# Extra weight slots that stay in the ring until the last outputs need them, and a read-back placed behind the last weight load

## The chip, the cores and the metric

One core of one Trainium2 chip runs the whole program in one launch. The metric is the time of the program on the device in microseconds; lower is better. The notes below call the engines by the profile's names: PE (matrix multiplies), DVE (vector), ACT (scalar), POOL, and SP, whose queue issues nearly all of the transfers here.

## The reference

A two-layer network over 256 tokens and 256 context tokens of width 1024. Each layer is a mixer (a gated linear attention, a Fourier mix and a windowed attention, merged) and then a mixture of 16 experts. Layer 0 works on tokens and context (512 rows), layer 1 on the tokens alone. What matters here is the mixture, and the start of the mixer that follows it:

```python
def hierarchical_moe(h, w_router_group, w_router_expert, w1, w3, w2):
    ...                                   # one group of four, two experts in it, their gates
    for e in range(MOE_EXPERTS):
        hid = jax.nn.silu(h @ w1[e]) * (h @ w3[e])
        out = out + (hid @ w2[e]) * gates[:, e:e + 1]
    return out
...
k_a, v_a, k_c, v_c, q_a, r_a, u_b, q_c, gate_logits = split_by(h @ w_in, IN_SIZES)
```

All weights are float32: an expert has 6 MB of them (`w1` and `w3` 1024 x 512, `w2` 512 x 1024).

## The kernel before, in words

In the mixture the experts stand in 16 places. Each place computes only the tokens that were routed to it: up to 128 rows in a big place ("B" in `PLACES`), up to 64 in a small one ("s"). The last two places, 14 and 15, are small in both layers. A big place splits its weights into a high and a low part on ACT and DVE; a small one multiplies the float32 weights as they are. The outputs of places 0 to 13 are scattered by an indirect DMA on POOL into a buffer `yb` in device memory. The outputs of the last two places stay on the chip, in the tiles `yes` that `last_y` takes; one-hot matmuls (`put_rows`, L1776) bring their rows to the tokens. `rows(t)` reads `yb` back for a block of 128 tokens (L1760), POOL adds its two halves (L1761), an identity matmul adds the sum to the same PSUM bank (L1779), and DVE multiplies by the gate (L1797) and adds the result to `x` (L1799). Layer 0 has four such blocks (t = 0 to 3), layer 1 two. Between the two halves of this lies a branch (`tc.If`, L1785) for the rare case that a place overflows; every engine loads the counter `cnti`, compares and jumps. In this run the branch isn't taken.

The weights come in pieces of 1 MB, six to a place, 96 to a layer, all issued from SP (`wload`, L245). `pieces_of` gives their order: for each place the second half of `w1` and of `w3`, then the first halves of the next place, then the two halves of `w2` of this one. So the last four pieces of a layer, 93 to 96, are the second halves of `w1` and `w3` of place 15 and its two pieces of `w2`; 91 and 92 are `w2` of place 14.

`ring` hands out the slot of the next piece in turn. The ring has 8 slots in layer 0 (9 in layer 1), two of them the tiles of the pool `raw`, which the mixer's own loads use too. `moe_ahead` adds four extra slots, so that there are 12 (13). With 12 slots in turn, pieces 91 and 92 stand in the two `raw` tiles of layer 0. In the kernel before, `ring` drops every extra slot that it meets once 84 pieces have been handed out (`CUT`), and the list `spare` gives the dropped slots to the last two outputs and the first two read-backs.

A tile is reused only when its last reader is done: the load into it waits on a semaphore, on SP, and SP issues in order. The order of the instructions on each engine is made by a scheduler from the program's order and its priorities; `behind` adds an edge that keeps one instruction after another on the same engine.

Of the kernel before, what the change touches and what calls it, by code (L numbers as in the profile page):

```python
# [8 lines left out]
F32 = mybir.dt.float32  # L9
F32R = mybir.dt.float32r  # L10
# [9 lines left out]
P = 128  # L20
# [10 lines left out]
RING = (6, 7)  # L31
ONCE = (0, 2)
AHEADG = 2
CUT = 84
EXTRA = 2
EA = 8
EB = 1
# [77 lines left out]
def ts(i, n):  # L115
    return slice(i * n, (i + 1) * n)
# [12 lines left out]
class Net:  # L129
# [468 lines left out]
    def mixer(self, l, filler):  # L598
        nc, io = self.nc, self.io
# [19 lines left out]
        if l:  # L619

            h = [hp.tile([P, 2, KD, SEQ], F32R, name=n) for n in ("hhi", "hlo")]
# [16 lines left out]
        s1 = ExitStack()  # L638
        yc = self.swa(s1)
        self.dump(f"y2{l}", yc[0].bitcast(F32))  # L640
        self.rings, self.ahead, self.slots, self.piece, self.gen = [], [], [], 0, self.pieces_of(l)
        if l:

            self.rings = [(Slot(self.x[:, 2:4].rearrange("p t d -> p (t d)")), False)]
# [1 line left out]
            n = EXTRA  # L646
# [4 lines left out]
        yb = self.fourier(s1)  # L651
# [610 lines left out]

    def ring(self):

        self.piece += 1
        if self.piece > CUT:

            while self.rings[0][1]:
                self.rings.pop(0)
        self.rings.append(self.rings.pop(0))  # L1270
        return self.rings[-1][0].tile([P, 2048], F32, name="wraw")

    def pieces_of(self, l):

        def src(w, q):
            if q < STAT[l]:
                return self.io[w][l, q]
            if q not in self.eid:
                self.eid[q] = self.nc.values_load(self.idi[0:1, q:q + 1], engines=(mybir.EngineType.SP,),
                                                  min_val=0, max_val=NE - 1)  # L1280
            return self.io[w][l][bass.ds(self.eid[q], 1)].rearrange("e r c -> (e r) c")

        def up(w, q, c):
            return (w, q, c), self.wload(src(w, q)[ts(c, 512), :], 4, 512, self.ring())

        def down(q):
            for c in range(2):
                yield ("w2", q, c), self.wload(src("w2", q)[ts(c, 256), :], 2, 1024, self.ring())

        def begin(q):  # L1290
            for w in ("w1", "w3")[:1 + (PLACES[l][q] == "s")]:
                yield up(w, q, 0)
        self.eid = {}
        yield from begin(0)
        for q in range(NE):
            yield up("w1", q, 1)
            if PLACES[l][q] == "B":
                yield up("w3", q, 0)
            yield up("w3", q, 1)
            if q + 1 == STAT[l]:  # L1300
                yield from down(q)
            if q + 1 < NE:
                yield from begin(q + 1)
            if q + 1 != STAT[l]:
                yield from down(q)
# [68 lines left out]
    def moe_ahead(self, l):  # L1374


        n = 2 - l
        y1 = self.pool(self.sd, "rb1", bufs=n, side="right")
        y0 = self.pool(self.sd, "rb0", bufs=n, side="right")

        self.spare = self.once[1:] + [y0] * n + [y1] * n + self.once[:1]
        self.rings[2:2] = [(p, True) for p in self.spare]
        gen = self.pieces

        first = [next(gen) for _ in range(len(self.rings) - ROWS[l].count("w"))]
        last = self.wd
        for o in ROWS[l]:
            if o == "w":
                with self.tc.issue_after(last.ins):
                    first.append(next(gen))  # L1390
                last = self.wd
            else:
                self.behind(self.hw[int(o)], last)
                last = self.hw[int(o)]
        self.pieces = chain(first, gen)
        self.got, self.cut, self.parts = {}, {}, 6
        self.cut["w1", 0, 0] = list(self.halves("w1", 0, 0))

    def moe(self, l):
        nc, io, tc = self.nc, self.io, self.tc  # L1400
# [4 lines left out]
        dp, h2b, yb, lg = self.dp, self.h2b, self.yb, self.lg  # L1405
# [33 lines left out]
        i = V.tensor_add(Mb, O[:, 0], O[:, 1])  # L1439
# [17 lines left out]
        for t in range(nt):  # L1457
            i = V.tensor_scalar(self.oh0[:, t], self.iotab[:, :cap], pm0[:, t:t + 1], None, op0=OP.is_equal)
# [209 lines left out]

        def last_y(e):

            ye = self.spare.pop(0).tile([P, 2048], F32, name="wraw").bitcast(F32R).rearrange("p (h d) -> p h d", h=2)
            yes.append(ye)
            return ye
        p1 = begin(0, xx)
        for e in range(NE):
# [33 lines left out]
            if e == NE - 2:  # L1709
# [9 lines left out]
                rq = self.pool(sr, "rows2", bufs=2, side="right") if nt > 2 else None  # L1719
            if not big[e]:  # L1720
                p2 = self.c2()
                for c in range(2):
                    w = self.piece_at("w2", e, c)
                    for k in range(2):
                        pair(p2, hs, [w[:, k:k + 1, ts(o, 512)] for o in range(2)], (2 * c + k, 4), 1)
                if e < NE - 2:
                    ye = yp.tile([P, 512], F32, name="ye")
                    nc.scalar.activation(ye, p2, AF.Copy, scale=gsl[:, e:e + 1])  # L1728
                    put = (ye, e)
                    continue  # L1730

                ye = last_y(e)[:, :, :512]
                nc.scalar.activation(ye[:, 0], p2, AF.Copy, scale=gsl[:, e:e + 1])
                V.scalar_tensor_tensor(ye[:, 1], p2, gsl[:, e:e + 1], ye[:, 0].bitcast(F32), op0=OP.mult, op1=OP.subtract)
                continue
# [7 lines left out]
            if e < NE - 2:  # L1743
                ye = yp.tile([P, D], F32, name="ye")
                for o in range(2):
                    nc.scalar.activation(ye[:, ts(o, 512)], p2[o], AF.Copy, scale=gsl[:, e:e + 1])
                put = (ye, e)
                continue
            ye = last_y(e)
            for o in range(2):  # L1750
                q = ts(o, 512)
# [4 lines left out]

        def rows(t):

            yr = (self.spare.pop(0) if t < 2 else rq).tile([P, 2048], F32, name="wraw").rearrange("p (r d) -> p r d", r=2)
            nc.sync.dma_start(yr, yb.rearrange("(r q) d -> q r d", r=2)[ts(t, P)])  # L1760
            i = nc.gpsimd.tensor_add(yr[:, 0], yr[:, 0], yr[:, 1])  # L1761
            self.adds += [i] if t >= 2 else []
            return yr
        self.adds, self.lates = [], []
        yrs = [rows(t) for t in range(nt)]

        def put_rows(t, pt, js):
# [16 lines left out]
        n = nc.values_load(cnti[0:1, 0:1], min_val=0, max_val=T)  # L1784
# [3 lines left out]
        for t in range(nt):  # L1788
            self.pri.append(tc.cur_priority)
            yr = yrs[t]  # L1790
# [6 lines left out]
            i = [V.tensor_mul(yr[:, 1, ts(o, 512)], pt[o], gb[:, t // 2, ts(o, 512)]) for o in range(2)]  # L1797
# [118 lines left out]
```

## Time and profile before

| | us |
|---|---|
| three runs | 1570.74, 1577.3, 1569.88 (median 1570.74) |
| the profiled execution | 1564.04 |
| its span, first to last instruction | 1562.3 |
| end of layer 0's mixture, last output matmul of place 15 | 926.25 |
| first projection matmul of layer 1 | 950.34 |

Times in the profile run from the start of the span. The profiled execution is 6.7 us below the median of the three runs, and 1.7 us above its own span. A row of a timeline has the start, the duration, the engine, the line of the kernel, the operation, the tiles as output <- inputs, the count of instructions merged in it, and in brackets how long the engine was idle before it and what ended that. A float32 matmul leaves two records.

### The profile page before, as it was taken

The page shows a single profiled execution, that of the slowest core. Times are in us where ns is not written, and L with a number is a line of the kernel's source. Part 1 is how long each engine was busy: PE and PEld are TensorE (multiplying, and loading weights), DVE is VectorE, ACT ScalarE, POOL GpSimd, SP SyncE. Part 2 cuts the span into 40 slices and gives each one's busy share as a digit, 9 for nine tenths or more (in the row PEclk, how much of TensorE's full clock was granted, in tenths as well). Part 3 has the DMA queues.
Part 4 walks back from the last instruction along what each step waited for, and adds up shares of the span by engine and source line. Part 5 has one row for each costly group of instructions (what it writes and reads, how often), then busy time and mean ns, then how long its engine had stood idle before and what let it go on. Part 6 is the DMA issues. An engine that isn't in the chain of part 4 may idle for free. (4 is left out here: it accounts for less than half of the span.)

```text
span 1562.3 us, 22623 instructions
## 1 busy us (share of the span) xinstructions
PE 1437.5 (92%) x8333; PEld 1029.9 (66%) x8333; DVE 937.5 (60%) x1757; ACT 746.8 (48%) x1286; POOL 214.0 (14%) x238
## 2 busy tenths in 40 slices
PE   6999899999999998899999979999899979998885
PEld 4666666677777798676665428687689967553521
DVE  4379767432366786897776327467965689341412
ACT  4568556422223232576665306668654448341411
POOL 1124100000111101111111014023001111021001
PEclk9999999999999998999999988999999989999998
DMA  9772242543556578799999863322335699999992
GB/s 325 205 222 92 95 152 68 182 134 122 175 188 203 189 226 317 248 348 379 394 378 385 303 242 118 130 84 82 98 109 185 216 339 334 378 386 394 395 360 120
DMA packets 230795, 363.17 MB, mean 232 GB/s; under 512 B 25676, under 2 KB 125206, under 8 KB 230676
## 3 DMA queue, kind: packets, MB, share of 16 engines
q1 hardware_dynamic: 223808, 349.77, 64.2%
q0 software_dynamic: 6432, 11.76, 2.1%
q8 instruction: 69, 1.13, 0.3%
q14 instruction: 50, 0.41, 0.1%
q10 hardware_dynamic: 436, 0.10, 0.0%
HBM read 350.56 MB, written 21.82 MB: 238 GB/s over the span
## 5 line engine op out<-in xcount | busy, mean ns | idle before, releaser
L266 DVE TENSOR_TENSOR wlo<-wraw,whi 128x1024 fp32r<-128x1024 f32 (+1 forms) x324 | 377.9, 1180 | 184.8 <-ACT whi L265 126.7
L265 ACT ACTIVATE whi<-wraw 128x1024 fp32r<-128x1024 f32 (+1 forms) x324 | 322.3, 1010 | 258.6 <-PE pa L229 110.4
L228 PE MATMUL pa<-hhi,whi 128*128 128x512 f32 (+1 forms) x704 | 240.0, 356 | 1.9 <-ACT qT L795 1.0
L229 PE MATMUL pa<-hlo,whi 128*128 128x512 f32 (+1 forms) x704 | 237.7, 352 | 0.0
L228 PEld LDWEIGHTS pa<-hhi,whi 128*128 128x128 f32 x704 | 133.3, 189 | 27.9 <-issue 10.0
L231 PE MATMUL pa<-hhi,wlo 128*128 128x512 f32 (+1 forms) x704 | 150.5, 349 | 0.0
L1646 PE MATMUL pa<-wraw,xh 128*64 128x512 f32 x520 | 147.2, 626 | 0.0
L229 PEld LDWEIGHTS pa<-hlo,whi 128*128 128x128 f32 x704 | 133.4, 190 | 19.4 <-issue 6.5
L231 PEld LDWEIGHTS pa<-hhi,wlo 128*128 128x128 f32 x704 | 113.5, 190 | 19.2 <-issue 4.8
L1659 DVE SCALAR_TENSOR_TENSOR th<-th,pa 64x512 f32<-64x512 f32 (+1 forms) x32 | 21.7, 679 | 122.6 <-ACT th L1658 122.5
L770 POOL TENSOR_TENSOR m<-m,gu 128x512 f32<-128x512 f32 (+1 forms) x32 | 37.5, 1171 | 403.9 <-DVE gu L768 403.9
L1646 PEld LDWEIGHTS pa<-wraw,xh 128*64 128x64 f32 x520 | 43.7, 142 | 74.4 <-issue 71.3
L235 PE MATMUL pa<-whi,xh 128*128 128x512 f32 x208 | 84.9, 408 | 3.8 <-ACT whi L265 3.7
L236 PE MATMUL pa<-wlo,xh 128*128 128x512 f32 x208 | 85.8, 413 | 1.5 <-DVE wlo L266 1.4
L237 PE MATMUL pa<-whi,xl 128*128 128x512 f32 x208 | 83.6, 402 | 0.1
L1646 PE MATMUL c<-wraw,hh 128*64 128x512 f32 x256 | 69.3, 631 | 1.0 <-DVE hh L1702 1.0
L236 PE MATMUL pa<-y,whi 128*128 128x512 f32 (+1 forms) x192 | 66.3, 345 | 0.9 <-DVE y L272 0.9
L1558 POOL DMA_INDIRECT xg<-h2b,tki x30 | 33.4, 1113 | 242.6 <-PE c L1630 75.1
L235 PE MATMUL pa<-y,whi 128*128 128x512 f32 (+1 forms) x192 | 65.4, 341 | 0.7 <-DVE mx L1150 0.7
L237 PE MATMUL pa<-y,wlo 128*128 128x512 f32 (+1 forms) x192 | 64.9, 338 | 0.0
L359 DVE SCALAR_TENSOR_TENSOR adaw<-adaw,cT 128x512 f32<-128x512 f32 x56 | 45.3, 809 | 25.1 <-DMA adaw<-in_w_ada_dram 24.4
L1564 POOL DMA_INDIRECT yb<-ye,yki x28 | 28.4, 1013 | 220.0 <-ACT ye L1728 111.5
(456 smaller groups left out, 2792.0 us busy)
## 6 DMA issues: line engine op xcount, KB each, us to landing
wraw<-in_w_dram SPq DMA_DIRECT2D x184, 1024.0 KB
wraw<-in_w_in_dram SPq DMA_DIRECT2D x44, 1024.0 KB
adaw<-in_w_ada_dram SPq DMA_DIRECT2D x80, 512.0 KB
adaw<-in_w_ada_dram SPq DMA_DIRECT2D x8, 1024.0 KB
wraw<-in_w_out_dram SPq DMA_DIRECT2D x8, 1024.0 KB
x<-in_w_dram SPq DMA_DIRECT2D x8, 1024.0 KB
yb<-zero SPq DMA_DIRECT2D x12, 512.0 KB
wraw<-yb SPq DMA_DIRECT2D x6, 1024.0 KB
```

The source lines that it names most:

```text
L228: mm(out, lh, rh, start=(i == 0), stop=False)
L229: mm(out, lh, rl, start=False, stop=False)
L231: self.mm = mm(out, ll, rh, start=False, stop=(i == len(ops) - 1))
L235: mm(out, lh, rh, start=start, stop=False)
L236: mm(out, lh, rl, start=False, stop=False)
L237: self.mm = mm(out, ll, rh, start=False, stop=stop)
L265: self.sp = nc.scalar.activation(hv[:, :, q], v[:, :, q], AF.Copy)
L266: self.sl = self.lo.tensor_sub(lv[:, :, q], v[:, :, q], hv[:, :, q].bitcast(F32))
L359: nc.vector.scalar_tensor_tensor(v[:, j], v[:, j], ck, acc, op0=OP.mult, op1=OP.add)
L770: nc.gpsimd.tensor_add(self.m[:, j, :], self.m[:, j, :], u[:, :TY])
L1558: return nc.gpsimd.indirect_dma_start(out=xgs[e % len(xgs)][:n], out_offset=None, in_=h2b, in_offset=bass.IndirectOffsetOnAxis(ap=tki[:n, ...
L1646: nc.tensor.matmul(ps[ts(i, SM)], xs[:, k0[0] + k, :], w[:, k, :], start=(k0[0] + k == 0), stop=(k0[0] + k == k0[1] - 1))
```

## The change

`CUT`, the counter `piece` and the list `spare` go. The extra slots stay in the ring, and a new method `leave` takes the first extra slot in the ring's order out of it when it is needed: once for each of the last two outputs, once for each of the first two read-backs. The read-back DMA gets an edge that keeps it behind the last weight load (`self.wd`) on SP.

```diff
-CUT = 84
...
     def ring(self):
-        self.piece += 1
-        if self.piece > CUT:
-
-            while self.rings[0][1]:
-                self.rings.pop(0)
         self.rings.append(self.rings.pop(0))
         return self.rings[-1][0].tile([P, 2048], F32, name="wraw")
+
+    def leave(self):
+
+        i = next(i for i, r in enumerate(self.rings) if r[1])
+        return self.rings.pop(i)[0].tile([P, 2048], F32, name="wraw")
...
-        self.spare = self.once[1:] + [y0] * n + [y1] * n + self.once[:1]
-        self.rings[2:2] = [(p, True) for p in self.spare]
+        self.rings[2:2] = [(p, True) for p in self.once[1:] + [y0] * n + [y1] * n + self.once[:1]]
...
-            ye = self.spare.pop(0).tile([P, 2048], F32, name="wraw").bitcast(F32R).rearrange("p (h d) -> p h d", h=2)
+            ye = self.leave().bitcast(F32R).rearrange("p (h d) -> p h d", h=2)
...
-            yr = (self.spare.pop(0) if t < 2 else rq).tile([P, 2048], F32, name="wraw").rearrange("p (r d) -> p r d", r=2)
-            nc.sync.dma_start(yr, yb.rearrange("(r q) d -> q r d", r=2)[ts(t, P)])
+            yr = (self.leave() if t < 2 else rq.tile([P, 2048], F32, name="wraw")).rearrange("p (r d) -> p r d", r=2)
+
+            self.behind(nc.sync.dma_start(yr, yb.rearrange("(r q) d -> q r d", r=2)[ts(t, P)]), self.wd)
```

The change removes one line above most of the code, so a line of the kernel before has one or two less in the changed kernel. It also changes what the scheduler makes of the end of layer 0. On SP, before, from the last piece of place 14 on (`wraw_8257`; `wraw_8266` and `wraw_8268` are pieces 93 and 94, `wraw_8292` and `wraw_8298` pieces 95 and 96, `yb0_105` is `yb`):

```order
L245 DMA wraw_8257<-in_w2_dram 128x2x1024
...
L245 DMA wraw_8266<-in_w1_dram 128x4x512
...
L245 DMA wraw_8268<-in_w3_dram 128x4x512
...
L245 DMA wraw_8292<-in_w2_dram 128x2x1024
...
L245 DMA wraw_8298<-in_w2_dram 128x2x1024
L1760 DMA wraw_8308<-yb0_105 128x2x1024
L1760 DMA wraw_8311<-yb0_105 128x2x1024
L1760 DMA wraw_8314<-yb0_105 128x2x1024
L1760 DMA wraw_8317<-yb0_105 128x2x1024
L1784 TENSOR_LOAD cnti_5802
L1785 COMPARE_AND_BRANCH
```

And now (`wraw_9034` is the first load of layer 1's projection weights, into the `raw` tile in which piece 91, the first half of `w2` of place 14, stood):

```order
L244 DMA wraw_8257<-in_w2_dram 128x2x1024
L1783 TENSOR_LOAD cnti_5802
L1783 ISA x2
L244 DMA wraw_9034<-in_w_in_dram 128x8x256
...
L244 DMA wraw_8266<-in_w1_dram 128x4x512
...
L244 DMA wraw_8268<-in_w3_dram 128x4x512
...
L244 DMA wraw_8292<-in_w2_dram 128x2x1024
...
L244 DMA wraw_8298<-in_w2_dram 128x2x1024
L1759 DMA wraw_8308<-yb0_105 128x2x1024
L1759 DMA wraw_8314<-yb0_105 128x2x1024
L1759 DMA wraw_8311<-yb0_105 128x2x1024
L1784 COMPARE_AND_BRANCH
```

Layer 1's load, which stood behind the branch, now stands ahead of the last four weights of layer 0. The read-back of block 1 (`wraw_8311`) has gone behind that of block 2, and the fourth (`wraw_8317`) behind the branch.

On PE, before, from the last matmuls of place 15 to the branch (`c_8291` is that place's output, `ident` rows are the identity matmuls of blocks 0 and 1):

```order
L1646 MATMUL c_8291<-wraw,hh 64x512 x8
L1776 MATMUL pa<-wraw,oh 128x512 x2
L1776 MATMUL c_8322<-wraw,oh 128x512
L1776 MATMUL c_8323<-wraw,oh 128x512
L1776 MATMUL pa<-wraw,oh 128x512 x2
L1779 MATMUL pa<-wraw,ident 128x512 x2
L1776 MATMUL c_8322<-wraw,oh 128x512
L1776 MATMUL c_8323<-wraw,oh 128x512
L1779 MATMUL c_8322<-wraw,ident 128x512
L1779 MATMUL c_8323<-wraw,ident 128x512
...
L1784 TENSOR_LOAD cnti
```

And now:

```order
L1644 MATMUL c_8291<-wraw,hh 64x512 x8
L1775 MATMUL pa<-wraw,oh 128x512 x2
L1775 MATMUL c_8322<-wraw,oh 128x512
L1775 MATMUL c_8323<-wraw,oh 128x512
L1783 TENSOR_LOAD cnti
```

The identity matmuls of blocks 0 and 1 have gone behind the branch, as they stand in layer 1 in both kernels.

On DVE, before, what follows the branch:

```order
L1799 TENSOR_TENSOR x<-x,wraw 128x1024 x2
L414 TENSOR_SCALAR rsr<-ss 128x1
L532 TENSOR_SCALAR xr<-x,rsr 128x1024
L414 TENSOR_SCALAR rsr<-ss 128x1
L532 TENSOR_SCALAR xr<-x,rsr 128x1024
```

And now:

```order
L1796 TENSOR_TENSOR wraw<-pa,gb 128x512 x2
L1798 TENSOR_TENSOR x<-x,wraw 128x1024
L413 TENSOR_SCALAR rsr<-ss 128x1
L531 TENSOR_SCALAR xr<-x,rsr 128x1024
L1796 TENSOR_TENSOR wraw<-c_8322,gb 128x512
L1796 TENSOR_TENSOR wraw<-c_8323,gb 128x512
L1798 TENSOR_TENSOR x<-x,wraw 128x1024
L413 TENSOR_SCALAR rsr<-ss 128x1
L531 TENSOR_SCALAR xr<-x,rsr 128x1024
```

The gate multiplies of both blocks have moved behind the branch, and those of block 1 behind the normalised rows `xr` of block 0. In layer 1 only the names of the slots change on PE and SP, and no instruction passes another on any engine.

## Rows read from the trace of the kernel before

**Rows 1.** The page: busy time, share of the span and instructions of each engine.

```profile
PE 1437.5 (92%) x8333; PEld 1029.9 (66%) x8333; DVE 937.5 (60%) x1757; ACT 746.8 (48%) x1286; POOL 214.0 (14%) x238
```

**Rows 2.** All waits of PE, 880 to 935 us: us, times, longest.

```profile
PE c L1665 <- DVE th L1660: 4.8, 2, 2.9
PE pa L1776 <- DVE th L1659: 2.1, 1, 2.1
PE pa L1776 <- ACT wraw L1733: 1.6, 2, 0.8
PE c L1646 <- DVE hh L1702: 0.5, 1, 0.5
```

**Rows 3.** All waits of PE, 1484 to 1541 us, the end of layer 1.

```profile
PE c L1665 <- DVE th L1660: 7.7, 3, 2.9
PE pa L1776 <- DVE th L1659: 2.0, 1, 2.0
PE pa L1776 <- ACT wraw L1733: 0.8, 1, 0.8
...
```

**Rows 4.** What SP issues from 889 to 960 us: last weights, read-backs, layer 1's loads.

```profile
892.88 5.52 SPq L245 DMA_DIRECT2D wraw<-in_w_dram  x4
902.32 2.00 SPq L1760 DMA_DIRECT2D wraw<-yb  x4
918.44 38.50 SPq L245 DMA_DIRECT2D wraw<-in_w_in_dram  x3
```

**Rows 5.** Waits of SP's queue, 880 to 922 us.

```profile
SPq L245 <- PE c L1646: 16.2, 2, 15.1
```

**Rows 6.** Timeline of PE around places 13, 14 and 15 of layer 0.

```profile
890.12 0.59 PE L1646 MATMUL c<-wraw,hh 128*64 128x512 f32 x1
...
906.63 0.86 PE L1646 MATMUL c<-wraw,hh 128*64 128x512 f32 x1
...
913.58 3.65 PE L1646 MATMUL pa<-wraw,xh 128*64 128x512 f32 x14
...
921.04 5.21 PE L1646 MATMUL c<-wraw,hh 128*64 128x512 f32 x16 [0.52 <-DVE hh L1702]
```

**Rows 7.** One lone load of 1 MB: issue; DMA, 956 to 964 us in 40 slices.

```profile
956.58 0.37 SPq L245 DMA_DIRECT2D wraw<-in_w_in_dram  x1
DMA  0000000067275999999999999410000069667999
GB/s 0 0 0 0 0 0 0 0 118 82 51 133 200 307 338 384 374 384 389 379 394 389 389 379 343 169 41 0 0 0 0 10 87 92 118 210 205 323 353 369
```

**Rows 8.** Stretches: busy time of each engine, granted clock (PEclk), DMA share, GB/s.

```profile
907.20:917.00 9.80, 8.97 (x40) 2.76 (x36) 0.75 (x1) 0.69 (x1) 4.72 (x2) 1.00 0.95 377
920.90:924.20 3.30, 3.16 (x8) 1.00 (x10) 0.09 (x1) 0.00 (x0) 0.00 (x0) 0.50 1.08 383
900.40:907.10 6.70, 6.23 (x18) 2.21 (x20) 0.75 (x2) 0.00 (x0) 0.00 (x0) 0.50 1.02 408
```

**Rows 9.** ACT and DVE after place 15 of layer 0, and eight identity matmuls.

```profile
926.31 0.69 ACT L1733 ACTIVATE wraw<-c,gsl 128x512 fp32r<-128x512 f32 x1 [7.79 <-PE c L1646]
936.21 2.36 DVE L1799 TENSOR_TENSOR x<-x,wraw 128x1024 f32<-128x1024 f32 x2 [2.89 <-DVEq L1785]
939.50 0.75 DVE L532 TENSOR_SCALAR xr<-x,rsr 128x1024 f32<-128x1024 f32 x1 [0.69 <-POOL rsr L415]
946.49 4.41 PE L1779 MATMUL c<-wraw,ident 128*128 128x512 f32 x8
```

**Rows 10.** ACT and DVE after place 15 of layer 1.

```profile
1540.85 0.69 ACT L1733 ACTIVATE wraw<-c,gsl 128x512 fp32r<-128x512 f32 x1 [6.22 <-PE c L1646]
1550.33 1.22 DVE L1799 TENSOR_TENSOR x<-x,wraw 128x1024 f32<-128x1024 f32 x1
1551.47 1.28 DVE L1797 TENSOR_TENSOR wraw<-c,gb 128x512 f32<-128x512 f32 x2
```

**Rows 11.** The stretch of layer 1's mixer, columns as in rows 8.

```profile
951.00:1180.00 229.00, 217.80 (x1520) 181.68 (x1519) 156.59 (x331) 149.35 (x311) 36.16 (x56) 1.00 0.36 115
```

More of the change, by code (lines that the diff above doesn't have):

```diff
@@ L640, in mixer @@
         self.dump(f"y2{l}", yc[0].bitcast(F32))
-        self.rings, self.ahead, self.slots, self.piece, self.gen = [], [], [], 0, self.pieces_of(l)
+        self.rings, self.ahead, self.slots, self.gen = [], [], [], self.pieces_of(l)
         if l:
```

## The prediction

> **What bounds the kernel now.** I read the page's engine table first: PE is busy 92% of the span [rows 1], so what counts is what makes PE wait or run slowly. Then the waits of PE at the two places that the change touches, the end of layer 0 and the end of layer 1. There PE waits 4.8 + 2.1 + 1.6 + 0.5 = 9.0 us and 7.7 + 2.0 + 0.8 = 10.5 us for its three longest, always for a vector or scalar result (`th`, `hh`, the output in `wraw`), never for a DMA [rows 2, 3]. So the last weights of a layer are there in time now. That fits the issues: pieces 93 to 96 of layer 0 leave SP from 892.88 to 892.88 + 5.52 = 898.40 us [rows 4]. The load that starts with the first of them sets out late: SP's longest wait, 15.1 us, is for the slot that piece 93 goes into [rows 5]. Yet PE starts on pieces 93 and 94 only at 913.58 (the `pa` matmuls of place 15) and on 95 and 96 at 921.04 [rows 6].
>
> A lone load shows how long 1 MB takes: issued at 956.58, its packets fill the DMA engines at 375 to 394 GB/s and fall off in the slices from 961.2 to 961.6 [rows 7], where a slice is 0.2 us. So it has landed about 4.75 us after the issue, and at 385 GB/s each further MB behind it takes 1.0486 / 0.385 = 2.72 us. By this piece 94 was there by about 898.4 + 4.75 + 2.72 = 906 at the latest, 7 us before it was needed.
>
> **The change, part by part.**
>
> *The slots that stay longer.* The 15.1 us wait of SP [rows 5] goes: in a ring of 12, piece 93 takes the slot of piece 81 and not that of 85. That is worth nothing by itself, since it hides behind the 7 us of slack just worked out. Its bounds: below nothing it could cost only if the earlier loads delayed another one that PE waits for, and there is none in [rows 2]; above, it can't give more than load waits of PE, and these are 0.
>
> *Layer 1's load ahead of four weights (term A).* This comes from the order. In the changed kernel the first `in_w_in` load stands on SP ahead of pieces 93 to 96. It goes into the `raw` tile of piece 91, the first half of `w2` of place 14. So it has to wait until PE has read that piece for the last time, and SP issues in order: behind the waiting load stand the four weights of place 15, the three read-backs and the branch. PE's pair of `w1`/`w3` matmuls of place 15 waits for the weights; POOL's sums wait for the read-backs.
>
> When does the wait end? A wait of this kind is in the trace: piece 93 now waits for the first half of `w2` of place 13, a small place too. That place's first output matmul starts at 890.12 [rows 6] and the load leaves at 892.88 [rows 4], 2.76 us later. Place 14's first output matmul starts at 906.63 [rows 6], for its first half microsecond still at a granted clock of 0.50, then at 1.00 [rows 8]; 0.86 us in place of 0.59 for the first record adds 0.3. So `in_w_in` leaves at 906.63 + 2.76 + 0.3 = 909.7. It has landed at 909.7 + 4.75 = 914.4; piece 93 follows at 917.1 and piece 94 at 919.9, the queue's four issues being shorter than the transfers. The matmuls of a pair take `w1` and `w3` in turn, so the first of them needs piece 93 and the second piece 94. PE was to start at 913.58 and starts at about 920: a stall of 6.3 to 6.6 us. Pieces 95 and 96 land at 922.6 and 925.3, while PE is in the pair and its `hh` step (7.5 us from pair to output now, 913.58 to 921.04), so they cost nothing. Bounds: with the three loads sharing the engines without any gap, and the issue 0.3 earlier, 5.9; with the slow rise of [rows 7] paid once more, 7.2. I take **6.6**.
>
> The Trainium skill, "DMA: Bandwidth & Descriptors", section "Anatomy of one DMA — SWDGE (gpsimd) path", gives about 2.0 us fixed plus bytes over 436 GB/s. By it the load takes 4.4 us and each further one 2.4, piece 94 lands at about 918.9, the stall is 5.3 and the sum below 10.6 in place of 11.9. This case's lone load took 4.75 at 385 GB/s, on SP's queue and not on that section's, so the row is used.
>
> *The clock behind the stall (term B).* After short lulls of PE here the granted clock fell from 1.00 to 0.50 (2.4 to 1.2 GHz) for 6.7 us (900.4 to 907.1) and for 3.3 us (920.9 to 924.2) [rows 8]. In the second of these, part of the outputs of place 15 already runs at half speed: 5.21 us for its 16 records [rows 6]. After 6.6 us without work the pair will start at 0.50 as well. 14 of its 16 records took 3.65 us at 1.00 [rows 6, 8]; at 0.50 the pair costs up to 3.6 more, and with the shortest stretch, 3.3 us, half of that, 1.7. The lower bound is 0, if the loss only moves from the later stretch to this one. I take **2.3**.
>
> *The identity matmuls behind the branch (term C).* The three read-backs leave SP later (they leave at 902.32 now [rows 4]) but have time until place 15 ends. What is behind the end changes its order. Before, in layer 0: from ACT's output of place 15 at 926.31 to the end of DVE's additions to `x` for both blocks, 936.21 + 2.36 = 938.57, is 12.3 us [rows 9]. Layer 1 already has the new order: 1540.85 to 1550.33 + 1.22 = 1551.55, 10.7 us, for block 0 alone [rows 10]. Then, by DVE's order, comes `xr` of block 0, which before ended at 939.50 + 0.75 = 940.25 (and there both additions were over 1.7 before) [rows 9], so some 2.8 after its own addition; then two multiplies, 1.28, and the addition of block 1, 1.22 [rows 10]. That is 10.7 + 2.8 + 2.5 = 16.0 against 12.3: block 1's rows come 3.7 later, and with them the transposes and the projection. A part may come back, since the eight identity matmuls of blocks 2 and 3, 4.41 us now [rows 9], may meet the full clock. Bounds: 1.5 (most of that back, and PE with block 0's rows to work on) to 4.5. I take **3**. The fourth read-back, now behind the branch, feeds those later blocks, which are done on PE only from 946.49 [rows 9]; I count it at nothing, inside these bounds.
>
> *Layer 1's end.* Only slot names change there, and PE waits for no load there [rows 3]: 0. What layer 0 loses isn't caught up in layer 1's mixer, where PE is busy 217.8 of 229.0 us at full clock [rows 11].
>
> **Sum:** 6.6 + 2.3 + 3 = 11.9 us; from the lowest bounds 5.9 + 0 + 1.5 = 7.4, from the highest 7.2 + 3.6 + 4.5 = 15.3. The profiled execution before took 1564.0, so 1576 for one like it. The median of the runs shown is 1570.7, 6.7 above: on that scale **1582.5**, with 1578 to 1586 as this case's own range.
>
> **The rivals.**
> *Not slower, the load is free early.* If the `in_w_in` load leaves 6.6 us sooner, by 903.1, nothing stalls. The place is SP's wait for piece 91's slot; 903.1 is the point from which it decides. For it speaks only that I had to tell from the order which slot it takes; against it that place 14's outputs don't begin before 906.63 [rows 6]. A gentler form: PE's lull is paid now and given back, since in the stall DVE and ACT, for which PE waits 9.0 us here [rows 2], catch up. But the waits for `th` and `hh` are inside a place's own chain and come after its pair. Left is term C or less: 0 to +3, so 1571 to 1574. Within 0.5%.
> *Faster, late weights are the real wait.* If the lulls put down to DVE's `th` (4.8 and 7.7 us, [rows 2, 3]) were in truth loads that came last, both go with longer-lived slots, 12.5 us: 1558. Against it: no DMA is named in either list, and the weights are there 7 us ahead. In its favour a general rule alone: the Trainium skill, "Trainium Kernel Development and Optimization", Best Practices, says "Double-buffer for performance: Overlap DMA with compute", by which more slots would help; the rows show the overlap complete already, so it has little weight here.
> *Slower by more.* Read-backs, issued behind piece 96 at about 913 to 925, come while the weights still move, and POOL's sums come later than the branch; or the half clock lasts through the outputs of place 15 as well (another 1.5 to 3 us). 15 to 18 us: 1586 to 1589.
>
> **How the numbers follow.** A measurement of this kernel can tell about 0.5%, 7.9 us, from no change. The forecast gets 0.75, slower by more 0.10, not slower 0.12, faster 0.03; 0.03 of the forecast's case lies under 7.9 us. So: faster 0.03, within 0.5% 0.15, slower 0.82. The range, 1574 to 1589, takes in the forecast's case, the longer one and the edge of the third; outside lie the faster case and most of the unchanged one.
>
> **What the profile after would show.** SP issues one `in_w_in` load at about 909.7, after a wait for PE, and right behind it the four weights. PE waits 6 to 7 us for a DMA ahead of the pair of place 15, which starts at about 920, and runs that pair at 0.50. The identity matmuls of blocks 0 and 1 stand behind the branch, and the first projection matmul of layer 1 is at about 962 where it was at 950.3 (the table above). Layer 1 takes as long as before. I am wrong if the load leaves well before 909, if the pair starts before 918, if no DMA is named among PE's waits, or if layer 1's end becomes shorter.

## The result, and the profile after

The changed kernel takes 1589.86 us (median of three runs, 1586.12 to 1593.5), the kernel before 1570.74: 1.012 of its time, with a 95% interval of 1.0076 to 1.0164, so 12 to 26 us slower. Measured again in six runs (below) it is 1.0081 (1.0053 to 1.0108), 8 to 17 us. The direction is as forecast; the first median lies 0.9 us above the top of the range. The profiled executions differ by 1584.3 - 1562.3 = 22.0 us.

The engine table of the changed kernel hardly differs from [rows 1], so the place has to be found by stretches:

```profile
PE 1450.4 (92%) x8333; PEld 1033.1 (65%) x8333; DVE 939.3 (59%) x1757; ACT 747.0 (47%) x1286; POOL 214.5 (14%) x238
```

The five largest waits of PE from 880 to 1000 us in the changed kernel (us in total, times, longest):

```profile
PE c L1663 <- DVE th L1658: 4.8, 2, 2.9
PE pa L1644 <- DMA wraw<-in_w_dram: 4.6, 2, 3.9
PE pa L543 <- DVE xr L531: 4.2, 2, 3.5
PE pa L1775 <- PEq L1784: 3.5, 1, 3.5
PE pa L1775 <- DVE th L1657: 2.1, 1, 2.1
```

Set it against [rows 2]: the waits for `th` are the same to a tenth, and a wait for a DMA has come, in the matmuls of a pair (L1644). What SP issues says why (start, duration, the count of merged issues at the end):

```profile
910.22 0.38 SPq L244 DMA_DIRECT2D wraw<-in_w_in_dram  x1
910.81 2.57 SPq L244 DMA_DIRECT2D wraw<-in_w_dram  x4
927.35 13.74 SPq L1759 DMA_DIRECT2D wraw<-yb  x4
```

The waits of SP's queue from 880 to 945 us say for what: the load of layer 1 for the last read of piece 91, the read-backs for PE's work on place 15:

```profile
SPq L244 <- PE c L1644: 19.2, 1, 19.2
...
SPq L1759 <- PE c L1644: 6.7, 1, 6.7
SPq L1759 <- PE pa L1644: 6.5, 1, 6.5
```

In [rows 4] the four last weights left from 892.88. Now they leave from 910.81, right behind layer 1's load, and the read-backs from 927.35 in place of 902.32. PE's timeline from there, and ACT's rows for place 14 (the first), the start of `th` of place 15 and the output of place 15:

```profile
918.10 1.97 PE L1644 MATMUL pa<-wraw,xh 128*64 128x512 f32 x2 [3.91 <-DMA wraw<-in_w_dram]
920.79 6.52 PE L1644 MATMUL pa<-wraw,xh 128*64 128x512 f32 x14 [0.72 <-DMA wraw<-in_w_dram]
931.36 6.36 PE L1644 MATMUL c<-wraw,hh 128*64 128x512 f32 x16 [0.52 <-DVE ssum L785]
962.18 4.59 PE L1778 MATMUL c<-wraw,ident 128*128 128x512 f32 x8
966.20 0.68 PE L227 MATMUL pa<-hhi,whi 128*128 128x256 f32 x1
```

```profile
911.94 0.69 ACT L1731 ACTIVATE wraw<-c,gsl 128x512 fp32r<-128x512 f32 x1 [10.54 <-PE c L1644]
927.40 0.59 ACT L1695 ACTIVATE th<-pa 64x512 f32<-64x512 f32 x1 [14.77 <-PE pa L1644]
...
937.77 0.69 ACT L1731 ACTIVATE wraw<-c,gsl 128x512 fp32r<-128x512 f32 x1 [9.16 <-PE c L1644]
```

The same ACT rows in the kernel before (the third is in [rows 9], 926.31):

```profile
911.39 0.69 ACT L1733 ACTIVATE wraw<-c,gsl 128x512 fp32r<-128x512 f32 x1 [12.09 <-PE c L1646]
917.31 0.59 ACT L1697 ACTIVATE th<-pa 64x512 f32<-64x512 f32 x1 [5.23 <-PE pa L1646]
```

With these rows the tail of layer 0 falls into three parts that no later part can disturb: **pair** (ACT's output of place 14 to `th` of place 15), **outputs** (`th` to ACT's output of place 15) and **after** (from there to layer 1's decay matmuls, the first with `wdraw`, which every block's rows must reach). Before: 5.92, 9.00 and 55.88 us, 70.80 in all. Changed: 15.46, 10.37 and 61.65, 87.48 in all. So 16.7 of the 22.0 us are in this tail: 9.5, 1.4 and 5.8. The other 5.3 are, to rounding, 0.5 ahead of it, 1.4 in layer 1 up to its place 14, 3.0 from there to place 15 and 0.5 behind. The experiments show differences of this size where the instructions are the same, so these aren't put down to the change.

### The profile page after: what moved, and what is told of

It is laid out like the page before. It is cut to its first block, busy times and chain, and to the rows that moved or that the text cites. A ratio compares the mean times of both kernels' runs of the same rounds, so it can differ in the third digit from the quotient of the medians.

```text
span 1584.3 us, 22621 instructions
## 1 busy us (share of the span) xinstructions
PE 1450.4 (92%) x8333; PEld 1033.1 (65%) x8333; DVE 939.3 (59%) x1757; ACT 747.0 (47%) x1286; POOL 214.5 (14%) x238
## 5 line engine op out<-in xcount | busy, mean ns | idle before, releaser
L1644 PE MATMUL pa<-wraw,xh 128*64 128x512 f32 x528 | 151.1, 637 | 4.6 <-DMA wraw<-in_w_dram 4.6
L1644 PEld LDWEIGHTS pa<-wraw,xh 128*64 128x64 f32 x528 | 44.3, 144 | 85.0 <-issue 75.3
L1644 PE MATMUL c<-wraw,hh 128*64 128x512 f32 x248 | 70.9, 661 | 1.0 <-DVE hh L1700 0.5
```

The source lines that it names most:

```text
L1644: nc.tensor.matmul(ps[ts(i, SM)], xs[:, k0[0] + k, :], w[:, k, :], start=(k0[0] + k == 0), stop=(k0[0] + k == k0[1] - 1))
```

## The experiments

Theory F, after the result: all of the loss is in that tail and has one root, the order on SP, with the clock and the late identity matmuls behind it. The rivals: L, the new slots of layer 1 cost something too; R, the late read-backs are the price and the load ahead is harmless.

**1. The changed kernel again.** No edit.

> The changed kernel once more, in more rounds. Theory F (the loss is all in layer 0's end: layer 1's first load stands ahead of the last four weights, PE stalls, the clock falls, the identity matmuls come late; the 6 us that the one profile shows at layer 1's end are the clock of that execution): 12 to 17 us slower than before, so 1.008 to 1.011 times its time. Rival L (the new slots of layer 1 cost some 6 us as well): 18 to 22 us, 1.012 to 1.014.

Measured: 1.0081 (1.0053 to 1.0108), 12.7 us; the tail has 15.49, 10.39 and 61.57. To a tenth of a microsecond the same tail, in an execution that is 8 us shorter as a whole (span 1576.1). F is inside, L not; the first measurement spoke for L.

**2. Layer 1's load behind the read-backs.** In `rows` and in `wload`:

```diff
+            if t == 2:
+                self.guard = d
...
+        if self.guard is not None:
+            self.behind(self.wd, self.guard)
+            self.guard = None
```

> As changed, but layer 1's first projection load is kept behind the third read-back on SP. Theory F: PE doesn't wait for a DMA at place 15 any more (the pair starts within 1 us of its output of place 14, as before), 10 to 11 of the 15 us of layer 0's end are gone; what is left is the late identity matmuls, 3 to 5 us: 1.001 to 1.004. Rival L: 8 to 11 us, 1.005 to 1.007. Rival R (the read-backs that wait for late slots are the price, not the load): no change against the changed kernel, 1.009 to 1.012.

On SP the four weights now come first, then the read-backs, then layer 1's loads:

```profile
882.86 10.61 SPq L244 DMA_DIRECT2D wraw<-in_w_dram  x4
917.54 13.56 SPq L1762 DMA_DIRECT2D wraw<-yb  x4
931.15 38.21 SPq L244 DMA_DIRECT2D wraw<-in_w_in_dram  x5
```

Measured: 1.0046 (1.0027 to 1.0065), 7.2 us. No DMA is among PE's waits; the parts are 5.93, 9.01 and 61.57. Pair and outputs are as before to 0.01 us, so the load ahead of the weights makes the 9.5 us and, through the clock, the 1.4. Theory R, which expected no change, falls. But the third part stays at 5.7 us above before, more than the 3 to 5 that I expected, and the read-backs still leave late, from 917.54; experiments 8 and 9 show what that costs.

**3. The change in layer 1 alone, and 4. in layer 0 alone.** The old `ring` and `spare` without the edge for one layer, the new ones with it for the other.

> The whole change in layer 1 alone; layer 0 as before. Theory F: 0 within 3 us (0.998 to 1.002), and PE waits for no DMA in layer 1's end. Rival L: 5 to 7 us slower, 1.003 to 1.0045, with the same loss at the end of layer 1 as in the changed kernel's profile.

> The whole change in layer 0 alone; layer 1 as before. Theory F: the same as the changed kernel, 12 to 17 us slower, 1.008 to 1.011. Rival L: some 6 us less than the changed kernel.

Measured: layer 1 alone 0.9995 (0.9966 to 1.0023), layer 0 alone 1.0129 (1.0103 to 1.0154). The loss comes with layer 0's part, and the 5 to 7 us of L aren't there without it (up to 3.6 us lie in the interval). Layer 0 alone lies above the 1.008 to 1.011 that F expected, and above experiment 1. Its tail is 87.62, as in the changed kernel, so the surplus lies outside of the tail, and what makes it stays open. And in both profiles layer 1's last places took longer than in the first profile of the kernel before. The stretch of the last three places, 188 PE instructions, in the kernel before and in the two (columns as in [rows 8]):

```profile
1489.00:1544.00 55.00, 41.40 (x188) 13.70 (x186) 8.65 (x14) 8.33 (x14) 6.66 (x4) 1.00 0.73 278
```

```profile
1487.50:1549.00 61.50, 47.57 (x188) 15.31 (x186) 8.65 (x14) 8.39 (x14) 6.65 (x4) 0.88 0.74 284
```

```profile
1501.30:1564.00 62.70, 50.41 (x188) 16.10 (x186) 8.65 (x14) 8.34 (x14) 6.66 (x4) 0.84 0.64 243
```

The same work, the same DVE and ACT time; PE's busy time and the granted clock differ. The third row is of the kernel with the change in layer 0 alone, whose layer 1 is the one before.

**5. Without the edge.** `self.behind(..., self.wd)` of the read-back taken out, the slots as changed.

> The extra slots stay as in the changed kernel, but the read-backs aren't kept behind the last weight. In the order two read-backs then stand on SP ahead of pieces 93 to 96, and layer 1's first load is behind the branch again. Theory F (whatever stands ahead of pieces 93 and 94 and has to wait for something late makes PE wait): the two read-backs wait for the scatter of place 13, until about 902; piece 94 lands at about 902 + 4.75 + 3 x 2.72 = 915, so PE waits 1 to 2 us at place 15 and not 4.6 to 6.6; with the late identity matmuls (5.8 us in the run with the load behind the read-backs) 6 to 10 us in all at layer 0's end. Rival R (only a load into a slot still in use can do it): no wait for a DMA at place 15.

Measured: 1.0033 (1.0005 to 1.0061), 5.2 us; parts 5.94, 7.43 and 59.91. SP:

```profile
894.32 0.90 SPq L1759 DMA_DIRECT2D wraw<-yb  x2
895.48 4.15 SPq L244 DMA_DIRECT2D wraw<-in_w_dram  x4
```

Two read-backs do stand ahead of the weights, but their scatter was done at 894.1 and not at 902, so the four weights left some 15 us earlier than in the changed kernel and PE, which began the pair at 908.13, did not wait for them. The 1 to 2 us that I expected did not come: I had taken the time of the scatter from [rows 4]. There the read-backs did wait for it (the kernel before, SP, 880 to 922 us):

```profile
SPq L1760 <- DMA yb<-ye,yki: 3.9, 1, 3.9
```

But that scatter, issued on POOL at 895.57, ran beside the last weights (DMA share 1.03, 382 GB/s from 895.5 to 902.3) and took 6.7 us; here, issued at 891.65 with little else under way (0.14, 49 GB/s from 891.6 to 894.3), it took 2.4. R is not helped: it is no matter of the kind of transfer but of when what stands ahead may go. The two early read-backs are those of blocks 2 and 3; POOL's first sum still waits for a read-back that left at 911.82, and the third part is 4.0 above before.

**6. The edge alone, on the kernel before.**

> The kernel before with the edge alone (read-back behind the last weight). The order is the same on every engine, so this is the kernel before once more with a profile of its own. All theories: 1.000 within the measurement. On layer 1's end: theory F says that the first profile of the kernel before ran its last 50 us at an unusually good clock, so this one takes 6 to 7 us longer there, as all kernels since; rival L2 (something in all the changed kernels slows layer 1's end) says that it takes as long as in the first profile.

Measured: 1.0003 (0.9978 to 1.0029); tail 5.92, 8.96 and 56.07. So neither half of the change makes PE wait for a weight by itself (5 and 6). With both, as the orders read, slots that leave late make the read-backs late, the edge puts them behind the weights, and the scheduler moves the counter's load and layer 1's first load ahead; why it does so wasn't tested. The last three places took as long as in the first profile, at the same clock of 1.00. F was wrong in that. Rival L2 is not held up either, since experiment 8, whose layer 1 is the changed one, has the 14.2 us from output to output of the last two places that the kernel before has (17.2 in the changed kernel).

**7. Two loads ahead.** An edge that keeps piece 93 behind layer 1's second projection load too.

> As changed, with layer 1's second projection load also ahead of piece 93. It takes the slot of piece 92, which PE reads until about 912 us, so it leaves some 2.2 us after the first and moves behind it. Theory F: piece 94 lands one transfer, 2.7 us, later; the pair of place 15 starts 2.5 to 3 us later than in the changed kernel, the rest of the tail the same or up to 1 us shorter (that load is then there early). Rival R (the late read-backs are the price): nothing changes but the wait before the pair, and the end of layer 0 stays at 13.5 to 15 us.

```profile
921.75 1.97 PE L1649 MATMUL pa<-wraw,xh 128*64 128x512 f32 x2 [7.29 <-DMA wraw<-in_w_dram]
924.45 5.58 PE L1649 MATMUL pa<-wraw,xh 128*64 128x512 f32 x14 [0.73 <-DMA wraw<-in_w_dram]
...
933.85 3.65 PE L1649 MATMUL c<-wraw,hh 128*64 128x512 f32 x16 [0.52 <-DVE ssum L790]
```

Measured: 1.0101 (1.0064 to 1.0138). PE waits 7.29 + 0.73 in place of 3.91 + 0.72: 3.4 us more, somewhat over the one transfer expected. The pair part is 17.90, 2.4 more. But the outputs run at the full clock, 3.65 us for 16 records in place of 6.36, and the tail is 87.40, the same as with one load. That the longer stall brings the clock back earlier isn't shown: in experiment 12 (below), with one load ahead and the same 4.6 us of waiting as in the changed kernel, the outputs take 3.65 us too:

```profile
922.43 1.97 PE L1654 MATMUL pa<-wraw,xh 128*64 128x512 f32 x2 [3.87 <-DMA wraw<-in_w_dram]
...
934.51 3.65 PE L1654 MATMUL c<-wraw,hh 128*64 128x512 f32 x16 [0.52 <-DVE ssum L786]
```

Against that profile, whose tail is 83.8, the second load costs 3.6 us.

**8. The identity matmuls ahead of the branch.** Experiment 2, and for layer 0 the second half of `put_rows` and the gate multiplies for blocks 0 and 1 written ahead of `values_load`, with the counter's load kept behind them:

```diff
+            put_rows(t, pts[t], (0, 1) if first else (0,))
...
+                se.enter_context(tc.issue_after(self.lm.ins))
+                se.enter_context(tc.issue_after(g[1][1].ins))
```

> As the run with the load behind the read-backs, and in layer 0 the identity matmuls and gate multiplies of blocks 0 and 1 are kept ahead of the branch, as before the change. If the order behind the branch is what remains of layer 0's loss (5.8 us), 4 to 6 us of it go and 0 to 2 are left: 0.999 to 1.002. If it is that the second read-back comes late (it waits for the first half of w2 of place 15), PE waits for POOL's sum ahead of the branch, 3 us or more, and 3 to 5 us are left: 1.002 to 1.003.

Measured: 0.9978 (0.9955 to 1.0002); parts 5.93, 9.03 and 59.19. The third part falls from 61.57 to 59.19, and a new wait stands in PE's list:

```profile
PE c L1784 <- POOL wraw L1766: 1.4, 1, 1.4
```

So the order explains 2.4 of the 5.7 us, and 3.3 stay, the 3 to 5 of the second case of the expectation. But PE's wait is 1.4 us and not 3 or more, and the total is below both cases (for that see experiment 9).

**9. Early slots.** Experiment 8, with the slots of the first two read-backs taken, in layer 0, at the output of place 14 (`yrt.extend([self.leave(), self.leave()])` in `last_y`).

> As the run with the identity matmuls ahead of the branch, and the slots of the first two read-backs leave the ring already at the output of place 14, so that no read-back waits for PE's work on place 15. Theory F: what was left of layer 0's tail there (3.4 us from ACT's output of place 14 to layer 1's decay matmuls) is the late second read-back (1.4 us of waiting for POOL ahead of the branch, and block 1 late behind it); 3 us of it go and the tail is as before, 70.8 within 1 us; 0.996 to 1.001 of the kernel before. Rival O (the rest is the changed order on DVE and ACT behind the branch): the tail stays at 73 to 74.

Measured: 0.9949 (0.9928 to 0.997), 8 us faster than before; parts 5.94, 10.27 and 56.29. The third part is back within 0.4 us of before, and 55.89 in experiment 11, which has the same order there. The tail, 72.5, is outside of the expected 70.8 within 1, since the outputs took 10.27 at a lower clock; in experiment 11 it is 70.75. The read-backs leave together again:

```profile
887.76 6.40 SPq L244 DMA_DIRECT2D wraw<-in_w_dram  x4
898.78 2.00 SPq L1764 DMA_DIRECT2D wraw<-yb  x4
```

In experiment 8 they took from 912.17 to 920.41. So the 3.3 us (2.9 in this profile) are the read-backs that wait for a slot which PE still reads; rival O falls by the two tails together. The split into 2.4 and 3.3 comes from taking away the order first and the slots second, with one profile of each. In experiment 5, which has both, the third part is 4.0 and not 5.7 above before, so the split isn't good to better than some 2 us.

That it's faster than before by 8 us has another source: the edges also changed the order in the middle of layer 0. There PE waited 2.7 us for gathered rows (`xg`) in the kernel before, and the wait isn't there in 8, 9 and 11. Matched instruction by instruction, each of the three gains some 4.5 us between 815 and 845 us of the kernel before. Part of that is the clock: from 832 to 840 us it was 0.57 in the kernel before and 1.00 in experiment 9, but it was 1.00 in experiments 1, 4 and 5 too, which keep the wait, and these gain 2.8. So 1.7 us are left that the new order alone can claim, and the rest of the 8 us isn't shown.

**10. Layer 1's identity matmuls ahead of the branch, in the kernel before, and 11. both.**

> The kernel before with one edit: in layer 1 too the identity matmuls and gate multiplies stand ahead of the branch. If behind the branch is where they cost, as in layer 0, the end from ACT's output of place 15 to the last instruction gets 2 to 4 us shorter: 0.997 to 0.999, which the total may not tell. If PE's 3.3 us of waiting for the branch covers nothing of theirs, since they then delay the branch itself: 0 to 1 us.

> The early slots and the identity matmuls ahead of the branch in both layers. Theory F: the sum of the two, 2 to 4 us below the kernel before, 0.996 to 0.999.

Measured: 0.9924 (0.9897 to 0.9951) and 0.9941 (0.9915 to 0.9968), 12 and 9 us faster than before, both below the expected 0.997 to 0.999 and 0.996 to 0.999; with experiment 9 they are the fastest three. ACT's output of place 15 in experiment 10 is this row:

```profile
1549.60 0.69 ACT L1733 ACTIVATE wraw<-c,gsl 128x512 fp32r<-128x512 f32 x1 [7.92 <-PE c L1646]
```

From it to the end of the span are 1568.3 - 1549.60 = 18.7 us; in the kernel before 1562.3 - 1540.85 = 21.5 [rows 10]. In experiment 11 they are 18.4. So 2.8 to 3.1 us of both gains are shown, the 2 to 4 that were expected of this end. The rest of experiment 10's 12 us isn't in its profile, which is an execution longer than its median; where it comes from stays open. Experiment 11 isn't faster than 10, so the two edits' gains don't add up in the total.

**12. Layer 0 alone, one more profile.**

> The kernel with the change in layer 0 alone, one more profile. Its layer 1 has the instructions of the kernel before, yet its first profile ran the end of layer 1 at a granted clock of 0.84 where two profiles of the kernel before show 1.00. If that clock is chance of an execution, it can come out anew here (1.00 in the stretch of the last three places, 55 us). If it follows from the program (from the instant at which layer 1's end begins, or from the load ahead of it), it is 0.84 within 0.02 and 62 to 63 us again.

```profile
1507.10:1566.00 58.90, 46.98 (x186) 15.11 (x185) 8.03 (x14) 8.37 (x14) 6.69 (x4) 0.88 0.73 276
```

Neither 1.00 nor 0.84 again: 0.88, 58.9 us. The same program has another clock there in another execution, as it has in the tail: outputs 7.44 us here, 10.42 in experiment 4 (parts 14.47, 7.44, 61.91; tail 83.8 and 87.6). From output to output of layer 1's last two places it has 15.9 us here and 17.2 there. So what layer 1's end takes isn't put down to the change, and a single profile is worth no more than some 4 us in such a stretch. That the kernel before had 1.00 there both times, and what decides it, stays open.

## Why the prediction was right and wrong

**The place and the chain were right.** The load was to leave at 909.7, and left at 910.22; the pair was to start in earnest at about 920, and its second step starts at 920.79. A DMA is named among PE's waits, with 4.6 us and not the 6 to 7 forecast, since the first step starts at 918.10, when piece 93 is there. The pair runs in a stretch where the mean granted clock is 0.57:

```profile
914.00:918.00 4.00, 0.20 (x1) 0.00 (x0) 0.00 (x0) 0.00 (x0) 0.00 (x0) 0.80 1.06 398
918.00:928.00 10.00, 8.49 (x16) 2.00 (x16) 0.00 (x0) 0.59 (x1) 0.00 (x0) 0.57 0.74 288
```

**Terms A and B** together were 6.6 + 2.3 = 8.9; the pair part grew by 9.5. The start of the pair's second step went from 913.58 to 920.79, less the 0.55 by which place 14 ended later: 6.7 for A (the working gave 6.3 to 6.6). 14 records took 6.52 in place of 3.65: 2.9 for B.

The two steps of the pair, each let go by a landed piece, start 2.69 us apart, which is nearly the 2.72 of a further MB worked out from [rows 7]. An estimate from the Trainium skill, "DMA: Bandwidth & Descriptors", section "Anatomy of one DMA — SWDGE (gpsimd) path", by its bytes over 436 GB/s, would be 2.4 us; the trace of these loads on SP's queue, 2.69, does not agree, and it is what counts here. The lone load's fall-off in [rows 7] lies in the slices from 961.0 to 961.4, one earlier than the prediction reads, which moves its 4.75 by 0.2 us at most.

**The clock on the outputs was left out of the sum.** I counted on the outputs of place 15 to run as before, and put half clock there into the rival *Slower by more*. They took 6.36 in place of 5.21 [rows 6], the part 1.4 more. In experiments 7 and 12, with the stall too, the part is 7.43 and 7.44, 1.6 less than before. So this was a term whose sign isn't fixed, and it belonged into the range, not into a rival.

**Term C is the step that failed**: "I take 3", from 1.5 to 4.5. It is 5.8, above its upper bound, and 5.7 to 6.2 in each of the six profiles with this tail (the changed kernel and experiments 1, 2, 4, 7, 12). The working itself, 3.7 us for block 1's rows, was within a microsecond. DVE's rows:

```profile
948.01 1.23 DVE L1798 TENSOR_TENSOR x<-x,wraw 128x1024 f32<-128x1024 f32 x1
...
953.34 1.22 DVE L1798 TENSOR_TENSOR x<-x,wraw 128x1024 f32<-128x1024 f32 x1
...
956.68 2.83 DVE L531 TENSOR_SCALAR xr<-x,rsr 128x1024 f32<-128x1024 f32 x1 [0.68 <-POOL rsr L414]
```

Block 1's addition ends at 954.56, 16.8 us behind ACT's row (16.0 worked out, 12.3 before), and the first projection matmul is 4.4 later. One thing that failed is the discount from 3.7 to 3, that "a part may come back" with the eight identity matmuls: they took 4.59, as against 4.41 [rows 9], and gave nothing back. Then 1.4 us more went in the first 33 us of the projection; the later blocks came late there, but that this is the reason isn't shown. The other thing is the wait of the read-backs, put at nothing because they "have time until place 15 ends". The slots that `leave` hands them hold weights of place 15: the first left at 927.35, behind PE's pair, and that of block 1 at 935.08, when the outputs had read the first of their two pieces. By experiments 2, 8 and 9 this was the larger part, some 3.3 of the 5.7 us, and the order 2.4.

**The scale.** The forecast was set on the median, 6.7 us above the profiled execution. The profile of the same program in experiment 6 lasts 1567.2 us. With A to C at their measured sizes and the outputs, 16.7, the forecast on that scale would have been 1587. The six runs of experiment 1 put the loss at 12.7 us, near the 11.9 of the sum, but that nearness is luck: the same tail, 16.7 us longer, stands in that execution as well, and the rest of the program moves by several us from one execution to the next (ACT's output of place 14 stands at 911.94 in the first profile and at 906.63 in this one).

**The rivals.** Neither *Not slower* nor *Faster* came: the load did not leave by 903, and PE's waits for `th`, 4.8 us, are what they were. *Slower by more*, at a chance of 0.10, named two mechanisms that did come, read-backs behind piece 96 and half clock on the outputs, and its 15 to 18 us take in the 16.7 of the tail. That layer 1's end would cost 0 holds for the total in experiment 3.

## What to carry to other kernels

A queue that issues in order makes a prefetch for the next stage harmful when its buffer frees late and urgent loads stand behind it: look in the issue order for the first load of the next stage, and at what its buffer still serves. Slots that are kept longer for loads are paid by whoever takes them next; here the two read-backs lost some 3 us in slots that were still read, and taking those slots one place earlier gave it back. Work that a scheduler lets slip behind a branch can be held ahead of it, which was worth some 2.4 us in layer 0 and 3 us at the end of layer 1. Before a gain in one stretch is put down to an edit, look at the clock of that stretch in several profiles of the same program: here it moved single stretches by 3 to 4 us.

## What the runs showed of the hardware

The granted clock behind a lull isn't a fixed price: the same 16 output matmuls of place 15 took 3.65 us behind a stall of 8.0 us (experiment 7), and behind one of 4.6 us once 6.36 (changed kernel) and once 3.65 (experiment 12). In two executions of one program (4 and 12) the part that they stand in took 10.42 and 7.44 us. Over the last three places of layer 1, with the same 188 PE instructions, 55.0 to 62.7 us were seen, at mean clocks from 1.00 to 0.84. The scatter of place 13 took 2.4 us with the DMA engines at a share of 0.14 (experiment 5) and 6.7 us beside weight loads at 1.03 (the kernel before). Two loads of 1 MB, one right behind the other on SP's queue, let go of PE 2.69 us apart.
